# Pinning the splits of h between weight splits in the down projection, and spreading the turning of x2 over three steps

## The chip, the cores and the metric

The kernel runs on one core of a Trainium2 chip. The metric is the time of one execution in microseconds (us) of device time. Before the change it is 2275.61 us, the median of three runs (2274.94 to 2275.78). One further execution was taken with the hardware profiler; its trace is what the numbers of this document come from, unless a run is named.

## The reference, cut to what matters

One decoder layer on 512 tokens of width 2048: a mixing layer, cross attention to 256 memory tokens, and a SwiGLU feed-forward layer of width 5632. The change touches only the end of the last one:

```python
hf = rms_norm(x, g_ffn)
gg, uu = jnp.split(hf @ w_gu, 2, axis=-1)
return x + (jax.nn.silu(gg) * uu) @ w_down
```

Below, h is `silu(gg) * uu`, and x2 is the `x` that is added at the end.

## The kernel before, in words

**Products in three parts.** A matrix is split into a high part in fp32r and a low part, the rest (`split`, L159: ScalarE casts to the high part, VectorE subtracts it to get the low part). A product is then three matmuls: high by high, high by low, low by high (`mm3`). Each split of a 128x1024 tile costs one ScalarE and one VectorE instruction.

**The down projection.** It is computed with seven block products (a Strassen scheme on a 2 by 2 block matrix) in four steps, `STEPS = ((6,), (0, 3), (4, 5), (1, 2))`. Step 0 has one product, the others two each. A step runs over `NK = 22` values of `kp`; for each kp and each product it does four block pairs of three matmuls, so 12 matmuls per kp in step 0 and 24 in steps 1 to 3. The two first and the two last kp of a step are done together, block by block.

**Weights.** `load_w(step, kp)` issues the loads of a kp's weights on SyncE into one of three `raw` buffers and splits them into five `qh` (high) and four `ql` (low) buffers. In step 0 one call serves kp and kp + 1. It runs with priority `AHEAD = 150`: the planner that orders each engine's instructions ranks them as if they were written 150 instructions earlier. `done_split` holds the last weight split that was written.

**h.** The gate and up phases before leave h in DRAM, in `hd`, in 6 groups `GRP` of two 512-wide blocks (the last has one). A group serves four kp. `load_h(step, g)` has GpSimd load the group's combination for each product of the step into a `PB` buffer (there are 16), and `split_h(step, g)` splits it into two further PB buffers. If `SPLIT_AT` has an entry for the pair, the split isn't written with the load but later, in `late_splits`, right behind `load_w` of the step and kp of the entry; it must then be issued behind the last weight split written (`tc.issue_after`, an order on one engine without a wait). The last block of h is turned by `turn` in step 0, at kp 2 and 4 (VectorE transposes and sums, 32 small GpSimd writes to `hd`), and group 5 is loaded at kp 5.

Nothing but that lower limit and the priorities says where a late split of h goes in the engine's queue. An engine takes its instructions in the queue's order.

**x2.** The x that is added at the end lies in DRAM with features across partitions and has to be turned. It is done in 16 pieces: `load_piece` (SyncE load of 256 KB, which waits for the last weight split), `turn_piece` (a VectorE transpose behind the last weight split, then four GpSimd writes to `x2n`). `TURN_AT` lists the places; pieces are loaded two places ahead. `add_rows` adds rows of x2n into four 128x512 result tiles by GpSimd DMAs, at the places in `ROWS_AT`: columns 1024 to 2047 first, then the others.

Of the kernel before, what the change touches and what calls it, by code (L numbers as in the profile page):

```python
# [28 lines left out]
NK = NF // 2  # L29
# [31 lines left out]
def hybrid_block(ctx: ExitStack, tc: tile.TileContext, x_t, mem_t, sv, cmat, umask, w_a, w_r67, w_v, w_vg, w_v3,  # L61
# [26 lines left out]
    def bank(tag):  # L88
        return psp.tile([128, 512], F32, name=tag, tag=tag, bufs={"mm": 3, "s": 2, "t": 2, "o": 1}[tag])
# [66 lines left out]
    def split(hi, lo, src, gain=None):  # L156

        if gain is None:
            return S.copy(hi, src), V.tensor_sub(lo, src, hi)  # L159
        return (S.activation(hi, src, AF.Copy, scale=gain),  # L160
                V.scalar_tensor_tensor(lo, src, gain, hi, op0=OP.mult, op1=OP.subtract))
# [510 lines left out]
    done = set()  # L672
# [201 lines left out]
    w = Weights(w_r67, 4096)  # L874
# [205 lines left out]
    w = Weights(w_cq[1], 2048)  # L1080
# [7 lines left out]
    def sb1(tag, dt=F32):  # L1088
        return pool1.tile([128, COLS2.get(tag, 512)], dt, name=tag, tag=tag, bufs=BUFS2[tag])
# [7 lines left out]
    def split_cols(raw, a, n):  # L1097
        hi, lo = sb1("qh", F32R), sb1("ql", F32R)
        done_split[0] = split(hi[:, :n], lo[:, :n], raw[:, a:a + n])
        return hi, lo  # L1100
# [91 lines left out]
    def sb2(tag, dt=F32):  # L1192
        return pool2.tile([128, COLS2.get(tag, 512)], dt, name=tag, tag=tag, bufs=BUFS2[tag])
# [125 lines left out]
    def weights_a(kp):  # L1319
        p = kp + LAG  # L1320
        with tc.high_priority(offset=60):
            if p >= KP:
                if p not in both_raw:
                    both_raw[p] = raw = sb1("raw")
                    for i in range(2):
                        if kp + i < KP:
                            nc.sync.dma_start(raw[:, 1024 * i:1024 * i + 512], w_gu[0, kp + i, :, 1536:2048])
                            nc.sync.dma_start(raw[:, 1024 * i + 512:1024 * i + 1024], w_gu[0, kp + i, :, 0:512])
                            both_raw[p + i] = raw
                a = split_cols(both_raw[p], 1024 * ((p - KP) % 2), 1024)  # L1330
            else:
                a = split_cols(both_raw[p], 1024, 1024)
        return part(a, 0, 512), part(a, 512, 512)
# [61 lines left out]
    GRP = [range(g, min(g + 2, NB)) for g in range(0, NB, 2)]  # L1395
# [41 lines left out]
    for p in range(KP):  # L1437
        if 1 <= p < KP - 1:
            ws.append(co_weights(p + 1))
        if p >= LAG:  # L1440
            w = weights_a(p - LAG)
# [31 lines left out]
    quad = [(i, j) for i in range(2) for j in range(2)]  # L1473
    groups, dw = {}, {}

    SPLIT_AT = {(1, 3): (1, 6), (0, 2): (0, 4), (0, 3): (0, 6), (0, 4): (0, 10), (0, 5): (0, 18)}
    for s in (1, 2, 3):
        SPLIT_AT[s, 4], SPLIT_AT[s, 5] = (s, 10), (s, 14)
        if s > 1:
            SPLIT_AT[s, 0], SPLIT_AT[s, 1], SPLIT_AT[s, 2], SPLIT_AT[s, 3] = (s - 1, 18), (s, 2), (s, 4), (s, 6)  # L1480
    h_raw, h_split = {}, {}

    def split_h(step, g):
        n = 512 * len(GRP[g])
        for a in STEPS[step]:
            hi, lo = h_split.pop((a, g), None) or (sb2("PB", F32R), sb2("PB", F32R))
            split(hi[:, :n], lo[:, :n], h_raw.pop((a, g))[:, :n])
            groups[a, g] = hi, lo

    def load_h(step, g):  # L1490
        n = 512 * len(GRP[g])
        for a in STEPS[step]:
            raw = h_raw[a, g] = sb2("PB")
            r = 128 * SLOT[a] - 128
            G.dma_start(raw[:, :n], hd[g][r:r + 128])
            if step == 0:
                h_split[a, g] = sb2("PB", F32R), sb2("PB", F32R)
        if (step, g) not in SPLIT_AT:
            split_h(step, g)
# [81 lines left out]
    def late_splits(step, kp):  # L1581
        for (s, g), at in SPLIT_AT.items():
            if at == (step, kp):
                with tc.issue_after(done_split[0][0].ins), tc.issue_after(done_split[0][1].ins):
                    split_h(s, g)

    def load_w(step, kp):

        with tc.high_priority(offset=AHEAD):
            raw = sb1("raw")  # L1590
            x, y = raw[:, :1024], raw[:, 1024:]
            if step == 0:
                nc.sync.dma_start(x, w_down[3, kp])
                nc.sync.dma_start(y, w_down[3, kp + 1])
            elif step == 1:
                nc.sync.dma_start(x, w_down[0, kp])
                nc.sync.dma_start(y, tw.get((1, kp), w_down[1, kp]))
            elif step == 2:
                nc.sync.dma_start(raw, td[kp])
                x, y = y, x  # L1600
            else:
                nc.sync.dma_start(x, w_down[2, kp])
                nc.sync.dma_start(y, tw.get((3, kp), td[kp][:, 1024:]))
            w = [split_cols(raw, 0, 1024)]
            if step % 2 and (step, kp) not in tw:
                V.tensor_add(y, x, y)
            w.append(split_cols(raw, 1024, 1024))
            if step == 2:
                w.reverse()
            if step == 0:  # L1610
                dw[0, kp], dw[0, kp + 1] = w[:1], w[1:]
            else:
                dw[step, kp] = w
# [11 lines left out]
    x2n = dram.tile([T, D], F32, name="x2n", tag="x2n", bufs=1)  # L1625
    pieces = {}
    ORDER = [*range(8, KT), *range(8)]
    TURN_AT = [(step, kp) for step in (1, 2) for kp in range(2, 18, 2)]
    ROWS_AT = {(2, 3): ((0, 1), (1, 1)), (3, 3): ((0, 0), (1, 0))}

    def load_piece(p):
        if p < KT:
# [38 lines left out]
    def gather_all(*steps):  # L1671
        for s in steps:
            for x in range(4):
                gather(*s[:4], x, *s[4:])
# [6 lines left out]
    for step, plan in enumerate(STEPS):  # L1681
        rs_ = range(len(plan))
        if step == 0:
            banks[0] = banks[1]
        elif step == 1:
            banks = [[bank(t) for t in SETS[r]] for r in rs_]
        elif step == 2:
            banks[1] = [bank(t) for t in SETS[1]]
        else:
            banks = [[bank(t) for t in SETS[r]] for r in rs_]  # L1690
        at = 3 if step else 7
        for kp in range(NK):
            if step or kp % 2 == 0:
                load_w(step, kp)
                late_splits(step, kp)

            if kp in (1, NK - 1):
                for r in rs_ if kp == 1 or step == 2 else reversed(rs_):
                    for x in range(4):
                        for k in (kp - 1, kp):  # L1700
                            down_product(step, r, k, (x,))
                        if step == 3 and kp == NK - 1:
                            gather(ADD, *((0, 0), (1, 0))[r], banks[r], x, True, (r, x) == (0, 3))
            elif 1 < kp < NK - 2:
                for r in rs_:
                    down_product(step, r, kp, range(4))
            if step == 0 and kp in (2, 4):
                for go in turn(hs, NB - 1, kp // 2 - 1):
                    go()
            if step == 0 and kp == 5:  # L1710
                load_h(0, len(GRP) - 1)
            if (step, kp) in TURN_AT:
                p = TURN_AT.index((step, kp))
                for ahead in (0, 1, 2) if p == 0 else (2,):
                    load_piece(p + ahead)
                turn_piece(p)
            for which in ROWS_AT.get((step, kp), ()):
                add_rows(*which)
            if step < 3 and kp % 4 == 3 and kp >= at:
                load_h(step + 1, (kp - at) // 4)  # L1720
        if step == 0:
            load_h(1, len(GRP) - 2)
        if step < 3:
            load_h(step + 1, len(GRP) - 1)
        with tc.high_priority(offset=EVICT):
            if step == 0:
                for x in range(4):
                    S.copy(res[0, 1][x], banks[0][x])
            elif step == 1:
                for x in range(4):  # L1730
                    S.copy(res[1, 1][x], banks[1][x])
                gather_all((ADD, 0, 1, banks[1]))
                for x in range(4):
                    S.copy(res[0, 0][x], banks[0][x])
            elif step == 2:
                u = [sb2("C") for x in range(4)]
                for x in range(4):
                    S.copy(u[x], banks[0][x])
                gather_all((SUB, 0, 1, u))
                for x in range(4):  # L1740
                    ADD(u[x], u[x], banks[1][x])
        if step == 2:
            for x in range(4):
                store(x, 0, 1)
            gather_all((SUB, 1, 1, u, True))
            res[1, 0] = u
# [120 lines left out]
```

## Time and profile before

| | |
|---|---|
| median of three runs | 2275.61 us |
| profiled execution | 2274.64 us |
| its span in the trace | 2272.8 us |
| mean granted TensorE clock | 0.999 |
| TensorE's share of the chain that ended last | 94% |

The span runs from the program's first to its last instruction; the execution's time is 1.84 us longer. PE is TensorE, DVE VectorE, ACT ScalarE, POOL GpSimd, SP SyncE. A row of a timeline gives the start in us from the span's start, the duration, the engine, the line, what is written from what (a tile's name; PB<-PB is a split of h, qh<-raw and ql<-raw,qh are the two halves of a weight split, PB<-h is a load of h), how many instructions the row holds, and in brackets how long the engine was idle before and what ended that. A row of the waits gives us in total, how often, and the longest. PEclk is the granted share of TensorE's clock. The end of a matmul is modelled: one takes 0.39 us by its row and the next starts 0.23 us after it.

### The profile page before, as it was taken

To read this page: it belongs to the slowest core of one execution; us is meant where nothing else is said; L and a number is where in the kernel's file an instruction comes from. 1 tells how busy PE (TensorE), PEld (TensorE's weight loads), DVE (VectorE), ACT (ScalarE), POOL (GpSimd) and SP (SyncE) were. 2 spreads that over 40 slices of the span, in tenths; PEclk is the share of its full clock that TensorE was granted. 3 is DMA by queue.
4 is the path that set the end of the run, shared out by engine and by line. 5 is a ranking of instruction groups with operands and counts; after the bars stand their busy time and mean duration, and the time that the engine had idled before them with its cause. 6 is when DMAs were issued, how large, how long until landed. Compare 5 with 4: busy or idle time off the path is not lost.

```text
span 2272.8 us, 29839 instructions
## 1 busy us (share of the span) xinstructions
PE 2255.0 (99%) x10533; PEld 1869.5 (82%) x10533; DVE 1687.9 (74%) x2643; ACT 1157.5 (51%) x1759; POOL 441.8 (19%) x672
## 2 busy tenths in 40 slices
PE   9999999999999999999999999999999999999999
PEld 8988888888888888787888888888888877878887
DVE  6478865677785446698889888988898876776685
ACT  6334545566674336575555445544544545454452
POOL 0012100021110000110123323332333162223200
PEclk9999999999999999999999999999999999999999
DMA  6577656466645344595576657656765588899864
GB/s 199 137 190 183 168 158 175 126 169 176 153 165 187 131 138 137 195 247 177 170 208 199 177 178 207 199 172 180 209 195 173 174 286 297 294 290 318 285 220 148
DMA packets 136822, 442.60 MB, mean 195 GB/s; under 512 B 20160, under 2 KB 21184, under 8 KB 133728
## 3 DMA queue, kind: packets, MB, share of 16 engines
q1 hardware_dynamic: 82480, 306.83, 40.2%
q0 software_dynamic: 49440, 125.35, 22.7%
q10 hardware_dynamic: 4752, 8.52, 1.0%
q8 instruction: 82, 1.34, 0.2%
q14 instruction: 68, 0.56, 0.1%
HBM read 395.01 MB, written 98.30 MB: 217 GB/s over the span
## 4 chain that ended last, share of the span: by engine, by line
PE 94%; DMA 3%; DVE 2%; issue 1%; ACT 1%; POOL 0%; SPq 0%; DVEq 0%; ACTq 0%; POOLq 0%
PE mm L99 51%; PE t L99 17%; PE s L99 14%; PE o L99 10%; PE t L817 1%; DMA w<-w_c 1%; DMA PB<-h 1%; DMA h<-T 0%; DVE ql L159 0%; DMA w<-w_vsw 0%; DVE wl L159 0%; POOL h L1428 0%; ACT wh L159 0%; ACT qh L159 0%; DMA w<-w_a 0%
## 5 line engine op out<-in xcount | busy, mean ns | idle before, releaser
L159 ACT CAST qh<-raw 128x1024 fp32r<-128x1024 f32 (+1 forms) x526 | 510.9, 980 | 518.0 <-PE mm L99 130.8
L159 DVE TENSOR_TENSOR ql<-raw,qh 128x1024 fp32r<-128x1024 f32 (+1 forms) x526 | 589.3, 1129 | 129.5 <-PE mm L99 53.6
L99 PE MATMUL mm<-X,wh 128*128 128x512 f32 x1600 | 504.2, 395 | 0.0
L99 PEld LDWEIGHTS mm<-X,wh 128*128 128x128 f32 x1600 | 294.0, 188 | 56.3 <-issue 0.8
L99 PE MATMUL t<-qh,PB 128*128 128x512 f32 x968 | 333.3, 389 | 0.0
L99 PE MATMUL mm<-X,wl 128*128 128x512 f32 x800 | 313.6, 392 | 0.1
L99 PE MATMUL mm<-qh,PB 128*128 128x512 f32 x868 | 310.6, 391 | 1.7 <-ACT qh L159 0.9
L159 DVE TENSOR_TENSOR wl<-w,wh 128x1024 fp32r<-128x1024 f32 (+2 forms) x150 | 179.7, 1200 | 152.3 <-ACT wh L159 150.5
L159 ACT CAST wh<-w 128x1024 fp32r<-128x1024 f32 (+2 forms) x150 | 154.2, 1029 | 237.9 <-PE mm L99 174.8
L1428 POOL DMA_DIRECT2D h<-T x352 | 224.2, 702 | 218.8 <-DVE T L1408 175.4
L99 PE MATMUL s<-qh,PB 128*128 128x512 f32 x672 | 233.0, 392 | 7.0 <-ACT PB L159 4.2
L99 PE MATMUL mm<-qh,PA 128*128 128x512 f32 x640 | 219.9, 389 | 0.0
L99 PEld LDWEIGHTS t<-qh,PB 128*128 128x128 f32 x968 | 181.7, 188 | 37.9 <-ACT qh L159 0.2
L99 PEld LDWEIGHTS mm<-qh,PB 128*128 128x128 f32 x868 | 163.3, 188 | 37.2 <-ACT qh L159 2.3
L99 PE MATMUL t<-ql,PB 128*128 128x512 f32 x484 | 188.3, 389 | 0.0
L99 PE MATMUL o<-qh,PB 128*128 128x512 f32 x484 | 187.4, 389 | 0.0
L99 PEld LDWEIGHTS mm<-X,wl 128*128 128x128 f32 x800 | 150.2, 188 | 32.6 <-DVE wl L159 1.4
L99 PE MATMUL mm<-ql,PB 128*128 128x512 f32 x434 | 169.5, 391 | 0.1
L99 PEld LDWEIGHTS s<-qh,PB 128*128 128x128 f32 x672 | 126.1, 188 | 35.8 <-ACT PB L159 5.2
L99 PEld LDWEIGHTS mm<-qh,PA 128*128 128x128 f32 x640 | 120.2, 188 | 25.0
L99 PE MATMUL s<-ql,PB 128*128 128x512 f32 x336 | 131.2, 391 | 1.6 <-DVE ql L159 1.6
L99 PE MATMUL mm<-ql,PA 128*128 128x512 f32 x320 | 124.5, 389 | 0.0
(502 smaller groups left out, 3546.7 us busy)
## 6 DMA issues: line engine op xcount, KB each, us to landing
raw<-w_gu SPq DMA_DIRECT2D x88, 768.0 KB, 4.8
raw<-w_gu SPq DMA_DIRECT2D x88, 512.0 KB, 3.7
raw<-w_down SPq DMA_DIRECT2D x84, 512.0 KB, 5.3
td<-w_down POOLq DMA_DIRECT2D x66, 512.0 KB, 6.2
w<-w_a SPq DMA_DIRECT2D x60, 512.0 KB, 4.4
raw<-td SPq DMA_DIRECT2D x22, 1024.0 KB, 6.3
PB<-h POOLq DMA_DIRECT2D x35, 512.0 KB, 6.3
w<-w_out SPq DMA_DIRECT2D x32, 512.0 KB, 3.6
```

The lines of the kernel that those rows point to most:

```text
L99: last_mm[0] = PE.matmul(*args, **kw)
L159: return S.copy(hi, src), V.tensor_sub(lo, src, hi)
L817: PE.transpose(tp[:, 128 * (i - j):128 * (i - j) + 128], ps_[b][:, POFF[i] + 128 * j:POFF[i] + 128 * j + 128], ident)
L1428: queues[i].dma_start(rows[:, :, c:c + 32], src[32 * q:32 * q + 32, :, i])
```

## The change

1. `SPLIT_AT` places the splits of h for step 0: groups 2 to 5 now at kp 8, 12, 16 and 20, where they are first used (before: 4, 6, 10 and 18).
2. The weight split written next but one kp later (kp 10, 14, 18) must be issued behind that split of h, on ScalarE and on VectorE. Together with the existing `issue_after` this leaves the split of group 2 one place, between the weight splits of kp 9 and kp 10, and likewise for groups 3 and 4.
3. The loads of h for step 1 are written later in step 0: group 0 at kp 9 (before 7), group 1 at kp 17 (before 11), groups 2, 3 and 4 at the last kp (before 15, 19 and behind the loop).
4. The 16 pieces of x2 are turned at 5 places in step 1, 7 in step 2 and 4 in step 3 (before 8 and 8 in steps 1 and 2), and the rows are added at kp 12 of step 2 and kp 14 of step 3 (before kp 3 of each).

```diff
-    SPLIT_AT = {(1, 3): (1, 6), (0, 2): (0, 4), (0, 3): (0, 6), (0, 4): (0, 10), (0, 5): (0, 18)}
+    SPLIT_AT = {(1, 3): (1, 6), **{(0, g): (0, 4 * g) for g in range(2, len(GRP))}}
...
-    h_raw, h_split = {}, {}
+    h_raw, h_split, h_done = {}, {}, [None]
...
-            split(hi[:, :n], lo[:, :n], h_raw.pop((a, g))[:, :n])
+            done = split(hi[:, :n], lo[:, :n], h_raw.pop((a, g))[:, :n])
+            if step == 0:
+                h_done[0] = done
...
-            w = [split_cols(raw, 0, 1024)]
+            with ExitStack() as behind:
+                if step == 0 and (0, kp // 4) in SPLIT_AT and kp % 4 == 2:
+                    for i in h_done[0]:
+                        behind.enter_context(tc.issue_after(i.ins))
+                w = [split_cols(raw, 0, 1024)]
...
-    TURN_AT = [(step, kp) for step in (1, 2) for kp in range(2, 18, 2)]
-    ROWS_AT = {(2, 3): ((0, 1), (1, 1)), (3, 3): ((0, 0), (1, 0))}
+    TURN_AT = [(1, kp) for kp in range(4, 22, 4)] + [(2, kp) for kp in range(2, 21, 3)] + [
+        (3, kp) for kp in range(1, 11, 3)]
+    ROWS_AT = {(2, 12): ((0, 1), (1, 1)), (3, 14): ((0, 0), (1, 0))}
...
-        at = 3 if step else 7
...
-            if step < 3 and kp % 4 == 3 and kp >= at:
-                load_h(step + 1, (kp - at) // 4)
-        if step == 0:
-            load_h(1, len(GRP) - 2)
+            if step == 0:
+                for g in {9: (0,), 17: (1,), NK - 1: (2, 3, 4)}.get(kp, ()):
+                    load_h(1, g)
+            elif step < 3 and kp % 4 == 3:
+                load_h(step + 1, kp // 4)
```

## The prediction

> **What bounds the kernel now.** I read the page first, then busy time by stretches of the down projection, then TensorE's waits and its timeline, then the timelines of ScalarE, VectorE and GpSimd around each stall.
>
> ```profile
> span 2272.8 us, 29839 instructions
> PE 2255.0 (99%) x10533; PEld 1869.5 (82%) x10533; DVE 1687.9 (74%) x2643; ACT 1157.5 (51%) x1759; POOL 441.8 (19%) x672
> ```
> TensorE is the bound, so only its gaps can pay. The changed code runs from 1836.8 us on:
>
> ```profile
> core 0: us, PE busy (x) PEld busy (x) DVE busy (x) ACT busy (x) POOL busy (x), PEclk, DMA share, GB/s
> 1836.80:1858.50 21.70, 21.70 (x96) 17.67 (x95) 18.81 (x29) 10.14 (x11) 13.98 (x24) 1.00 1.02 364
> 1858.50:1874.50 16.00, 12.98 (x49) 10.05 (x48) 7.39 (x9) 5.16 (x5) 13.12 (x21) 0.89 0.74 199
> 1874.50:1888.60 14.10, 11.49 (x50) 9.09 (x50) 6.90 (x6) 7.08 (x8) 2.68 (x5) 1.00 0.77 283
> 1888.60:1906.30 17.70, 16.71 (x73) 13.22 (x72) 14.87 (x14) 11.59 (x13) 2.11 (x4) 1.00 0.79 292
> 1906.30:2026.00 119.70, 118.11 (x521) 97.47 (x521) 86.37 (x81) 56.20 (x60) 33.46 (x53) 1.00 0.85 292
> 2026.00:2146.00 120.00, 119.97 (x529) 98.68 (x528) 74.41 (x69) 60.08 (x62) 34.09 (x52) 1.00 0.90 298
> 2146.00:2260.00 114.00, 113.55 (x500) 93.32 (x499) 85.67 (x79) 51.18 (x51) 3.46 (x4) 1.00 0.60 205
> ```
> The first four rows are step 0; roughly, steps 1, 2 and 3 follow. TensorE idles 6.62 us in step 0 (3.02 + 2.61 + 0.99) and 1.59, 0.03 and 0.45 us in the others. The x2 part of the change lies in the stretches where little is lost. Here are the stalls of step 0:
>
> ```profile
> 1860.64 0.50 PE L99 MATMUL s<-qh,PB 128*128 128x512 f32 x1 [2.08 <-ACT PB L159]
> 1862.31 1.19 PE L99 MATMUL s<-qh,PB 128*128 128x512 f32 x2 [0.94 <-DVE PB L159]
> 1876.73 0.50 PE L99 MATMUL s<-qh,PB 128*128 128x512 f32 x1 [2.08 <-ACT PB L159]
> 1877.99 0.73 PE L99 MATMUL s<-qh,PB 128*128 128x512 f32 x2 [0.53 <-DVE PB L159]
> 1890.16 0.73 PE L99 MATMUL s<-qh,PB 128*128 128x512 f32 x2 [0.99 <-DVE PB L159]
> 1862.40:1865.80 3.40, 3.40 (x8) 2.72 (x9) 0.00 (x0) 0.00 (x0) 3.13 (x6) 0.50 0.95 313
> 1836.80 2.72 PE s L99 x12
> ```
> PB holds h. Twelve matmuls take 2.72 us undisturbed, so a pair of row blocks (kp k) would start at 1836.80 + 2.72k. I write w(k) for the split of its weights and h(s,g) for a group of h for step s; h(0,g) serves kp 4g to 4g+3. The stalls stand where h(0,2), h(0,3) and h(0,4) are first used. After the first, the granted clock is 0.50 for a stretch of 3.4 us.
>
> **Why h is late.** ScalarE's timeline, then one row of VectorE's, then GpSimd's:
>
> ```profile
> 1850.48 1.06 ACT L159 CAST qh<-raw 128x1024 fp32r<-128x1024 f32 x1 [1.71 <-DVE T L1418]
> 1853.15 1.06 ACT L159 CAST qh<-raw 128x1024 fp32r<-128x1024 f32 x1 [1.62 <-PE mm L99]
> 1858.59 1.04 ACT L159 CAST qh<-raw 128x1024 fp32r<-128x1024 f32 x1 [1.66 <-PE mm L99]
> 1859.54 1.04 ACT L159 CAST PB<-PB 128x1024 fp32r<-128x1024 f32 x1
> 1874.69 1.04 ACT L159 CAST qh<-raw 128x1024 fp32r<-128x1024 f32 x1 [1.66 <-PE mm L99]
> 1875.64 1.04 ACT L159 CAST PB<-PB 128x1024 fp32r<-128x1024 f32 x1
> 1882.90 1.05 ACT L159 CAST PB<-PB 128x1024 fp32r<-128x1024 f32 x1 [6.22 <-DMA PB<-h]
> 1883.86 1.05 ACT L159 CAST qh<-raw 128x1024 fp32r<-128x1024 f32 x1
> 1885.52 2.00 ACT L159 CAST PB<-PB 128x1024 fp32r<-128x1024 f32 x2 [0.61 <-DMA PB<-h]
> 1861.03 1.22 DVE L159 TENSOR_TENSOR PB<-PB 128x1024 fp32r<-128x1024 f32 x1
> 1842.81 1.11 POOL L1495 DMA_DIRECT2D PB<-h  x2
> 1847.65 0.53 POOL L1495 DMA_DIRECT2D PB<-h  x1 [3.73 <-PE mm L99]
> 1878.05 2.68 POOL L1495 DMA_DIRECT2D PB<-h  x5 [4.73 <-DMA h<-T]
> 1847.65 7.85 DMA PB<-h
> 1879.16 6.34 DMA PB<-h
> ```
> Five qh buffers let w(k) be cast only when kp k-5 is done. The cast at 1850.48 is therefore w(9) (kp 4 ends at 1850.40) and that at 1858.59 is w(12). h(0,2) stands behind w(12), at 1859.54, although it was issued at 1842.81 and, by the 7.85 us of h(0,4), had landed by about 1850.7. h(0,3) likewise stands behind w(16), at 1875.64. So the late thing is a place in ScalarE's queue, not a transfer. The third stall differs: h(0,4) is the second cast of the 1885.52 row, behind the two casts of h(1,0), of which the first held the queue 6.22 us for its transfer.
>
> **The sum, part by part.** The pins put h(0,2) between w(9) and w(10), h(0,3) between w(13) and w(14), h(0,4) between w(17) and w(18), on both engines. They add no instruction.
>
> Gain: idle time and the 3.4 us at half clock (worth 1.7 us) make 6.62 + 1.7 = 8.3 us. Restarts after a gap come on top, so I count matmuls: a matmul should take 2.72 / 12 = 0.2267 us, and one astride a seam between two windows is counted in both. The stretch of the first stall has 48 in 16.00 us, 16.00 - 10.88 = 5.1 us lost; the second 49 in 14.10, 14.10 - 11.11 = 3.0; the third 72 in 17.70, 17.70 - 16.32 = 1.4. Sum 9.5 us.
>
> Cover of the new places: w(9) ends at 1851.5 on ScalarE, h(0,2) follows for 1.04 us, before w(10) at 1853.15 is due, so that the added queueing costs w(10) nothing. VectorE subtracts w(9) when kp 5 is done (1853.1) and h(0,2) after it, 1.22 us each: done by 1855.6, needed at 1858.56, so 3.0 us to spare. The same sum holds for h(0,3) (needed at 1869.44), and for h(0,4), needed at 1880.32 and castable from about 1873.2, if h(1,0) is not ahead of it. w(10), w(14) and w(18) now wait behind h, and TensorE behind them; if a pinned h had not landed, each us of delay beyond 3.0 would cost a us. h(0,4) landed at 1855.50, long before.
>
> h(0,5), now behind w(21), is free when kp 17 is done, 1885.8, plus two subtractions: about 1888.2, against a need at 1891.20; its transfer, issued at 1878.05, by the 6.34 us of h(1,0)'s second one lands at 1884.4. Cover 3.0 us, cost 0.
>
> Moved loads: h(1,0) goes from kp 7 to kp 9. GpSimd issues it right behind h(0,5), which waits for block 10's writes to land (4.73 us), so its issue (second and third of the five at 1878.05) stays, and step 1 would begin at 1896.64, some 9 us after its two casts. h(1,1) is used 21.8 us into step 1 (four kp of 24 matmuls), h(1,2) and later 43 us and more: free. What is next late is h(1,0)'s first cast, landing at 1882.90, with w(18) or w(19) behind it: w(18) is due at 1885.76, and one cast and two subtractions end at 1882.90 + 1.05 + 2 x 1.22 = 1886.4, so 0.6 us lost; allowing as much again, I take 1.0.
>
> The x2 pieces:
>
> ```profile
> L1643 DVE STREAM_TRANSPOSE C<-C x16: 701/705/706, 1923.0 to 2111.3; 128x512 f32<-128x512 f32 x16
> L1647 POOL DMA_DIRECT2D x2n<-C x64: 649/649/710, 1924.0 to 2117.9; - x64
> L1652 POOL DMA_DIRECT2D C<-x2n x4: 849/1002/1382, 2147.7 to 2152.9; - x4
> DMA to landing us min/median/max: 4.6/9.3/17.7
> POOL x2n L1647 <- DVE C L1643: 106.3, 15, 15.4
> ```
> A piece is one SyncE load, a transpose of 0.705 us and four GpSimd writes of 0.649 us. GpSimd waits for each transpose, up to 15.4 us, with h's later loads behind; at 3 or 4 kp between pieces it can be 21.8 us, but a load written at kp 4g+3 is used at kp 4g of the next step, 19 kp (over 100 us) later. Four pieces enter step 3: 2.8 us of VectorE where it is busy 85.67 of 114 us, 10.4 us on an empty GpSimd. The load waits for the last weight split, and weight loads queue behind it on SyncE; three raw buffers cover that. The eight row additions of step 3 move to kp 14, about 2146 + 14 x 5.44 = 2222: eight issues of 1.0 us and 17.7 us to land give 2248, before kp 20 at 2254.8, where the last sums begin to need them. Step 2's additions, to kp 12, have 49 us. Cost 0, bounded by the one stall of step 1, 1.6 us, either way: it may go, as additions leave the start of step 2, or come again elsewhere.
>
> Sum: -9.5 + 1.0 + 0 = -8.5 us. The profiled execution took 2274.64 us (1.84 over its span), 0.97 under the median of 2275.61; from the median, 2267.1. Its own range, from -11.1 (no new delay, 1.6 us of step 1 too) to -5.5 (three us of cover lost), is 2264.5 to 2270.1. About 0.2%, 4.5 us, is what a measurement of this kernel can tell from no change.
>
> **The rivals.** *The stall moves to kp 16.* ScalarE keeps the order of the trace: h(1,0), w(17), h(1,0), h(0,4). For it: that order stands in the rows, h(1,0)'s load is still written ahead of h(0,4)'s split, and its transfer hangs on GpSimd, not on TensorE. Against: it arose while TensorE stood at h(0,3); without that stall w(17), h(0,4) and w(18) come free earlier, and the load is written two kp later. Then TensorE, free at 1880.32, waits for h(0,4) until the same 1887.5 and 1890.1 as now, gaining nothing, and a gap of 7 us would again bring 1.7 us of half clock in place of the old one, whose loss is absorbed: 0 to +1.7, so 2275.6 to 2277.3.
>
> [...]
>
> *The pins don't move the casts in time*: h(0,2)'s buffer is one that TensorE frees only when kp 7 ends. The row at 1859.54 shows no wait, but stands right behind one for TensorE, so this isn't excluded. No change, 2275.6.
>
> *Slower: both h(1,0) casts go ahead of w(14).* Deciding point: anything behind a cast that lands at 1885.50 (1879.16 + 6.34) and due before. w(14) would be cast at 1886.5 and subtracted by 1888.9, and kp 14, free at 1874.88, needs that for its second matmul: with half clock it starts in effect at 1888.9 - 0.2 + 1.7 = 1890.4. Now kp 16 starts in effect at 1890.16 - 0.45 = 1889.7 (the row is its third matmul), so kp 14 at 1889.7 - 1.4 - 5.44 = 1882.9. The third stall (1.4) would be gone: 7.5 - 1.4 = +6.1, so 2281.7. Against it: it needs the whole group to move up three weight splits.
>
> **How the numbers follow.** Forecast 0.60, stall moves to kp 16 0.22, pins idle 0.06, slower 0.12. Faster is the first, same the second and third, slower the last. The range 2264.5 to 2277.3 holds the first three, 0.88, less their tails.
>
> **What would show it.** Right: the first PB cast after 1850.48 follows w(9) directly and w(10) follows it; TensorE has no gap over 0.3 us between 1858 and 1880; the half clock stretch is gone; step 1's first matmuls come 8 to 9 us earlier. Wrong: a wait on PB near 1880 to 1890 with ScalarE waiting for PB<-h (the first rival), a wait of a PB cast for TensorE at 1858 (the second), or new idle time in steps 1 to 3 above 2 us.

## The result, and the profile after

The changed kernel is slower. Its median is 2288.22 us (2287.38 to 2291.08, five runs), against 2275.41 us (2274.94 to 2275.78, five runs) for the kernel before. The ratio is 1.0059, 95% interval 1.0044 to 1.0073. The forecast was 2267.1, and the range ended at 2277.3.

The profiled execution took 2288.06 us. Two lines of its page:

```profile
span 2286.3 us, 29838 instructions
PE 2255.3 (99%) x10533; PEld 1869.8 (82%) x10533; DVE 1686.7 (74%) x2643; ACT 1157.6 (51%) x1759; POOL 442.4 (19%) x672
```

TensorE's busy time and count are those of before (2255.0, 10533). The difference is idle time. Here are its waits from the start of the down projection to its end, first of the kernel before, then of the changed one (us in total, how often, the longest):

```profile
PE s L99 <- ACT PB L159: 4.2, 2, 2.1
PE s L99 <- DVE PB L159: 2.9, 4, 1.0
PE s L99 <- DVE ql L159: 1.6, 1, 1.6
```

```profile
PE s L99 <- ACT PB L159: 13.6, 1, 13.6
PE s L99 <- DVE PB L159: 3.7, 2, 2.3
PE mm L99 <- DVE ql L159: 1.7, 1, 1.7
```

Two waits for a cast of h have become one of 13.6 us, there is a new one for the low part of weights (`mm <- ql`), and the one of 1.6 us (`s <- ql`, between steps 1 and 2) is gone. Busy time by stretches shows where they lie; the down projection begins 3.33 us later than before, at 1840.13:

```profile
core 0: us, PE busy (x) PEld busy (x) DVE busy (x) ACT busy (x) POOL busy (x), PEclk, DMA share, GB/s
1840.13:1861.83 21.70, 21.70 (x97) 17.96 (x97) 21.28 (x34) 11.09 (x12) 13.93 (x24) 1.00 1.02 365
1861.83:1886.40 24.57, 10.95 (x50) 8.74 (x48) 4.58 (x4) 5.10 (x6) 15.17 (x25) 0.78 0.63 189
1886.40:1917.40 31.00, 29.64 (x120) 23.93 (x121) 21.44 (x20) 18.57 (x21) 2.12 (x4) 0.90 0.73 254
...
2157.00:2190.00 33.00, 29.01 (x127) 23.30 (x126) 23.23 (x24) 14.77 (x15) 8.73 (x12) 1.00 0.89 283
```

In the second row TensorE is busy 10.95 of 24.57 us; the last row, the first 33 us of step 3, has 4.0 us of idle time, where the kernel before had 0.45 us in the whole of step 3. ScalarE's timeline tells why step 0 stands still:

```profile
1853.81 1.06 ACT L159 CAST qh<-raw 128x1024 fp32r<-128x1024 f32 x1 [1.71 <-DVE T L1418]
1854.77 1.04 ACT L159 CAST PB<-PB 128x1024 fp32r<-128x1024 f32 x1
1856.49 1.06 ACT L159 CAST qh<-raw 128x1024 fp32r<-128x1024 f32 x1 [0.67 <-PE mm L99]
1859.21 1.06 ACT L159 CAST qh<-raw 128x1024 fp32r<-128x1024 f32 x1 [1.66 <-PE mm L99]
1861.93 1.06 ACT L159 CAST qh<-raw 128x1024 fp32r<-128x1024 f32 x1 [1.66 <-PE mm L99]
1882.13 1.04 ACT L159 CAST PB<-PB 128x1024 fp32r<-128x1024 f32 x1 [19.15 <-DMA PB<-h]
1883.09 1.04 ACT L159 CAST qh<-raw 128x1024 fp32r<-128x1024 f32 x1
1884.34 1.99 ACT L159 CAST PB<-PB 128x1024 fp32r<-128x1024 f32 x2 [0.22 <-DMA PB<-h]
```

The first row is w(9); h(0,2) follows it directly, then w(10), w(11) and w(12), as the pins say, and the first stall is gone. Behind w(12) stands h(1,0)'s first cast. It holds the queue for 19.15 us, until its data land. Only then come w(13), h(1,0)'s second cast and h(0,3), which kp 12 needs. GpSimd's timeline has the issue of that load, behind the writes of h's last block as before, and TensorE's timeline has the end of the wait:

```profile
1877.59 2.16 POOL L1497 DMA_DIRECT2D PB<-h  x4 [2.02 <-DMA h<-T]
```

```profile
1872.38 0.39 PE L99 MATMUL mm<-qh,PB 128*128 128x512 f32 x1
1886.39 0.79 PE L99 MATMUL s<-qh,PB 128*128 128x512 f32 x1 [13.62 <-ACT PB L159]
...
1888.97 1.22 PE L99 MATMUL s<-qh,PB 128*128 128x512 f32 x2 [1.36 <-DVE PB L159]
```

**A ledger of the down projection.** All these kernels execute the same 1848 matmuls of the down projection, in the same order but for 19 in the last two kp of step 0, so each matmul's start, counted from the first one of the down projection, can be compared with its start in the kernel before. The table gives that difference in us, for the changed kernel and all the experiments below, at six times of the kernel before: behind its three stalls (1874.0, 1888.6, 1906.3), at the end of step 1 and its stall (2026), before and behind the start of step 3 (2146, 2190), and at the end. "Starts" says how much later the down projection begins, where no edit here touches the code. Run 7 tells how far such numbers differ with no cause in the queues: up to 1.8 us.

| kernel | starts | 1874.0 | 1888.6 | 1906.3 | 2026 | 2146 | 2190 | end |
|---|---|---|---|---|---|---|---|---|
| the change | +3.33 | -5.21 | +9.24 | +7.76 | +6.20 | +6.19 | +10.10 | +10.09 |
| 1 without x2's part | +2.07 | -5.21 | +9.20 | +7.72 | +6.16 | +6.17 | +6.79 | +6.78 |
| 2 h(1,0) behind w(19) | +3.46 | -5.21 | -8.40 | -1.34 | -2.09 | -2.11 | -2.19 | -2.21 |
| 3 h(1,0) loaded early | +0.79 | -5.21 | -8.40 | -3.86 | -5.41 | -5.41 | -5.54 | -5.56 |
| 4 pins at the old places | +0.50 | -5.21 | -1.12 | +1.90 | +0.34 | +0.33 | +0.17 | +0.16 |
| 5 as 3, h(1,1) split later | +6.41 | -5.21 | -8.40 | -9.88 | -10.47 | -10.49 | -10.32 | -10.34 |
| 6 x2's part alone | +2.99 | +1.22 | +2.55 | +1.27 | -0.29 | -0.30 | +2.48 | +2.47 |
| 7 x2's additions alone (order as before) | +1.57 | +0.72 | +1.77 | +0.49 | -1.07 | -1.07 | -1.58 | -1.59 |
| 8 places without pins | +2.54 | -0.25 | +9.31 | +7.83 | +7.59 | +7.57 | +7.55 | +7.54 |
| 9 as 5, with x2's part | +2.54 | -5.21 | -8.40 | -9.88 | -9.75 | -9.77 | -6.14 | -6.16 |
| 10 as 3, h(1,1) loaded later | +1.18 | -5.21 | -8.40 | -9.88 | -11.42 | -11.43 | -10.82 | -10.83 |

For the changed kernel, 3.33 + 10.09 = 13.42 us is the whole difference of the two profiled executions (2288.06 - 2274.64). Step 0 gives 5.21 back, loses 14.45 (from -5.21 to +9.24) and ends at +7.76; step 3 loses 3.9 more.

### The profile page after: what moved, and what is told of

Its sections match the earlier page's. It is cut to its first block, busy times and chain, and to the rows that moved or that the text cites. A ratio compares the mean times of both kernels' runs of the same rounds, so it can differ in the third digit from the quotient of the medians.

```text
span 2286.3 us, 29838 instructions
## 1 busy us (share of the span) xinstructions
PE 2255.3 (99%) x10533; PEld 1869.8 (82%) x10533; DVE 1686.7 (74%) x2643; ACT 1157.6 (51%) x1759; POOL 442.4 (19%) x672
## 3 DMA queue, kind: packets, MB, share of 16 engines
q8 instruction: 82, 1.34, 0.2%
## 4 chain that ended last, share of the span: by engine, by line
PE 90%; DMA 3%; DVE 3%; issue 2%; ACT 1%; POOL 1%; SPq 0%; DVEq 0%; ACTq 0%; POOLq 0%
PE mm L99 50%; PE t L99 16%; PE s L99 13%; PE o L99 10%; DMA h<-T 1%; DMA PB<-h 1%; PE t L817 1%; POOL h L1428 1%; DVE wl L159 1%; DVE ql L159 1%; DMA raw<-w_down 0%; DMA w<-w_vsw 0%; ACT wh L159 0%; ACT qh L159 0%; DMA raw<-td 0%
## 5 line engine op out<-in xcount | busy, mean ns | idle before, releaser
L99 PE MATMUL s<-qh,PB 128*128 128x512 f32 x672 | 232.8, 391 | 17.3 <-ACT PB L159 13.6
```

The source lines that it names most:

```text
L99: last_mm[0] = PE.matmul(*args, **kw)
```

## The experiments

The theory after the result: what a split of h costs is set by what stands ahead of it on ScalarE, and h(1,0) came ahead of w(13) and h(0,3) because h(0,3)'s split is now written at kp 12, behind h(1,0)'s, which goes with its load at kp 9. (Before, it was written at kp 6, ahead of h(1,0) at kp 7, and stood ahead of it.) The rivals: the pins push weight splits back; the transfers are late in any order; the x2 part is what costs. Runs 1 to 4, 5 to 8, and 9 and 10 were each timed beside their own runs of the kernel before, whose medians were 2275.61, 2276.9 and 2275.06 us. Where the diff of a run doesn't say otherwise, it is against run 1.

**1. The change without x2's part.**

```diff
-    TURN_AT = [(1, kp) for kp in range(4, 22, 4)] + ...
-    ROWS_AT = {(2, 12): ((0, 1), (1, 1)), (3, 14): ((0, 0), (1, 0))}
+    TURN_AT = [(step, kp) for step in (1, 2) for kp in range(2, 18, 2)]
+    ROWS_AT = {(2, 3): ((0, 1), (1, 1)), (3, 3): ((0, 0), (1, 0))}
```

> The change without its x2 part: the pieces are turned and the rows added where they were before. Place theory (h(1,0)'s first cast stands on ScalarE behind w(12), ahead of w(13) and h(0,3), and holds them until its transfer lands near 1882 us): the 14 us gap at kp 12 and the half clock after it stay, ScalarE waits about 19 us for PB<-h; the time is the changed kernel's less what x2 costs there (about 2 us by the two traces: 3.9 lost in step 3, 1.9 gained between steps 1 and 2), so about 2286, 2283 to 2288. Rival (the x2 part with its transfers is what costs): near 2275 or below, and no such gap.

Measured: 2283.85 us, ratio 1.0033 (1.0022 to 1.0045). Step 0 is that of the changed kernel to 0.04 us. The loss at the start of step 3 shrinks from 3.9 us to 0.6. So the larger part of the loss is in step 0 and has nothing to do with x2.

**2. h(1,0) split at (0, 18).**

```diff
-    SPLIT_AT = {(1, 3): (1, 6), **{(0, g): (0, 4 * g) for g in range(2, len(GRP))}}
+    SPLIT_AT = {(1, 3): (1, 6), **{(0, g): (0, 4 * g) for g in range(2, len(GRP))}, (1, 0): (0, 18)}
```

> As e1, and one more entry places the split of h(1,0) behind w(19): only the place of two casts and two subtractions in their queues changes, no load moves. Place theory: no gap over 1.2 us in step 0, no half clock there; step 0 is 9.5 us shorter than before, at most 1 us given back where w(20) queues behind h(1,0): 2266 to 2268. Rival (the pins themselves hold the weight splits behind a late h): a gap of several us at kp 12 or 16 stays, 2280 or more.

Measured: 2273.96 us, ratio 0.9988 (0.9978 to 0.9997). The gap of 14 us is gone and so is the second stall (-8.40), with the pins in place: they aren't what costs. But the expected time is missed. ScalarE's timeline of this run:

```profile
1891.48 1.05 ACT L159 CAST PB<-PB 128x1024 fp32r<-128x1024 f32 x1 [9.33 <-DMA PB<-h]
1892.44 1.05 ACT L159 CAST qh<-raw 128x1024 fp32r<-128x1024 f32 x1
1893.94 2.00 ACT L159 CAST PB<-PB 128x1024 fp32r<-128x1024 f32 x2 [0.45 <-DMA PB<-h]
...
1898.69 0.61 ACT L159 CAST PB<-PB 128x512 fp32r<-128x512 f32 x1
```

The 128x512 cast is h(0,5), which kp 20 needs at about 1894.6; TensorE waits for it until 1899.35. Ahead of it stand h(1,0) and h(1,1), and the queue waited 9.33 us for the former to land. The same thing, one group further on.

**3. h(1,0) loaded at kp 1, split at (0, 10).** The load is now written ahead of the last block's writes to DRAM.

```diff
+    SPLIT_AT = {..., (1, 0): (0, 10)}
...
-                for g in {9: (0,), 17: (1,), NK - 1: (2, 3, 4)}.get(kp, ()):
+                for g in {1: (0,), 17: (1,), NK - 1: (2, 3, 4)}.get(kp, ()):
```

> As e1, but GpSimd loads h(1,0) at kp 1, ahead of the 32 writes of h's last block, and its split is placed behind w(11): its two casts keep a place ahead of w(13) and h(0,3) on ScalarE, yet their transfers land some 20 us earlier. Place theory (it is the wait for the transfer in that place that costs): the casts find their data, ScalarE waits for PB<-h under 2 us, no gap at kp 12; 2266 to 2270, with h(0,5) up to 2 us later. Rival (the place in itself, or the pins, cost whatever the transfer does): a gap of over 5 us stays, 2280 or more.

Measured: 2269.43 us, ratio 0.9969 (0.9955 to 0.9983). h(1,0) is still ahead, and costs nothing, because it has landed. What is left is a stall at kp 20; on ScalarE it is now h(1,1) that waits ahead of h(0,5), and 6.0 us are lost there, where the expectation allowed 2:

```profile
1889.42 1.05 ACT L159 CAST PB<-PB 128x1024 fp32r<-128x1024 f32 x1 [9.94 <-DMA PB<-h]
...
1893.21 0.61 ACT L159 CAST PB<-PB 128x512 fp32r<-128x512 f32 x1
```

**4. Pins with the splits at their old places** (4, 6, 10, 18); each group's pin is kept by its number.

```diff
-    SPLIT_AT = {(1, 3): (1, 6), **{(0, g): (0, 4 * g) for g in range(2, len(GRP))}}
+    SPLIT_AT = {(1, 3): (1, 6), (0, 2): (0, 4), (0, 3): (0, 6), (0, 4): (0, 10), (0, 5): (0, 18)}
...
-                h_done[0] = done
+                h_done[g] = done
...
-                    for i in h_done[0]:
+                    for i in h_done[kp // 4]:
```

> As e1, with the pins, but the splits of h for step 0 are written where they were before (kp 4, 6, 10, 18), so h(0,3) is written ahead of h(1,0). On ScalarE the first h(1,0) cast now stands behind w(16), the second behind w(17), then h(0,4). Place theory: the gaps at kp 8 and 12 go, and one at kp 16 takes their place (the first rival of the prediction): TensorE waits from 1880 until about 1887.5 and 1890, half clock again; 2275 to 2278. Rival (the pins cost in themselves): 2280 or more, gap at kp 12.

Measured: 2276.07 us, ratio 0.9999 (0.9991 to 1.0008). With h(0,3) written at kp 6 again, it stands ahead of h(1,0), and the second stall is gone too: TensorE has no gap at kp 12. (The table's -1.12 already holds most of the gap at kp 16, which begins at that very matmul; just before it the run stands at -8.40.) h(0,4), written at kp 10, is still behind h(1,0) at kp 9. ScalarE's timeline, h(1,0), w(17), then h(1,0) and h(0,4):

```profile
1883.38 1.04 ACT L159 CAST PB<-PB 128x1024 fp32r<-128x1024 f32 x1 [12.36 <-DMA PB<-h]
1884.33 1.04 ACT L159 CAST qh<-raw 128x1024 fp32r<-128x1024 f32 x1
1885.89 1.99 ACT L159 CAST PB<-PB 128x1024 fp32r<-128x1024 f32 x2 [0.52 <-DMA PB<-h]
```

This is the rival "the stall moves to kp 16" of the prediction, rows, place and price: nothing is gained.

**5. As run 3, with h(1,1) split at (1, 1)** and no longer at once with its load.

```diff
-    SPLIT_AT = {..., (1, 0): (0, 10)}
+    SPLIT_AT = {..., (1, 0): (0, 10), (1, 1): (1, 1)}
```

> This kernel is the change without its part on x2, with h(1,0) loaded at kp 1 and split at (0, 10) as in the run that loaded it early, and now also with h(1,1) split at (1, 1) and not at once. On ScalarE no cast of h(1,1) is then written ahead of the one of h(0,5). Theory (what counts is which cast of h stands ahead of which weight split): the gap at kp 20, which the early load left (2.2 us and 1.7 us of a half clock), goes as well, and all three stalls of step 0 are gone: 2275.6 - 9.5 = 2266.1, 2265 to 2268. Rival (the transfers of this stretch are the limit, so that whatever is split last is late in any order): a gap of 2 us or more stays at kp 16 or kp 20, and the time is that of the early load, 2269 to 2271.

Measured: 2269.21 us, ratio 0.9968 (0.9955 to 0.9981). The ledger has step 0 without any stall, 9.88 us shorter, and the down projection 10.34 us shorter; h(0,5) follows a weight split and waits for nothing:

```profile
1889.48 1.06 ACT L159 CAST qh<-raw 128x1024 fp32r<-128x1024 f32 x1 [1.66 <-PE mm L99]
1890.44 0.61 ACT L159 CAST PB<-PB 128x512 fp32r<-128x512 f32 x1
1892.20 1.06 ACT L159 CAST qh<-raw 128x1024 fp32r<-128x1024 f32 x1 [1.15 <-PE mm L99]
```

The theory holds for step 0. The time, 7.7 us under the median of before, is less than the down projection gained, no better than run 3's, and missed the expected 2265 to 2268. In the profiled execution the down projection began 6.41 us later, after a gap at 1571.00 to 1575.06 in which TensorE waited for weights of the gate and up phase. The changed kernel had such a gap at the same place (1571.53 to 1573.50), the kernel before and runs 1 to 4 had none.

**6. x2's part alone**, on the kernel before (the lines of run 1's diff, the other way round).

> The kernel before with only the change's part on x2: its pieces turned over steps 1 to 3, its additions at (2, 12) and (3, 14). The changed kernel stood 4.4 us above the change without this part (2288.2 and 2283.9). Theory (pieces and additions that meet the start of step 3 make the loads of weights land late there): the same cost shows alone, two gaps of 2 to 3 us at the start of step 3, some of it paid back by the gap between steps 1 and 2 that goes: 2277 to 2280. Rival (the cost arises only because step 0 ended later, with the writes of x2 then meeting other work): 2274.5 to 2276.5, no change.

Measured: 2277.96 us, ratio 1.0006 (0.9998 to 1.0015). The two gaps at the start of step 3 are there (+2.8 us from 2146 to 2190). The time is in the theory's range, but the interval goes from -0.5 to 3.4 us, so whether it costs time isn't settled by this run.

**7. x2's additions alone**, on the kernel before.

```diff
-    ROWS_AT = {(2, 3): ((0, 1), (1, 1)), (3, 3): ((0, 0), (1, 0))}
+    ROWS_AT = {(2, 12): ((0, 1), (1, 1)), (3, 14): ((0, 0), (1, 0))}
```

> The kernel before with only the places of x2's additions changed: (2, 12) and (3, 14) for (2, 3) and (3, 3); its pieces are turned where they were. If the additions are what delays the loads of weights at the start of step 3, this has the gaps of the whole x2 part there: 2277 to 2280. If the pieces that are turned and written in step 3 are what delays them, step 3 has no such gaps here, and the time is that of before or up to 2 us less (the 1.9 us gap between steps 1 and 2 may go with the additions): 2273.5 to 2276.

Measured: 2276.1 us, ratio 1.0001 (0.9991 to 1.001). No gap at the start of step 3 (-0.5 us). But the run doesn't test what it was meant to: the additions didn't move. TensorE, VectorE, GpSimd and SyncE execute the same instructions in the same order as in the kernel before, ScalarE too but for one swapped pair at 690 us; the additions stand here from 2020.9 to 2153.4 us, in the kernel before from 2020.4 to 2152.9. The entry in `ROWS_AT` alone doesn't decide their place. They do stand elsewhere in run 6, where the pieces are turned at other places. So it takes the pieces' new places, but whether by the pieces or by the additions that move with them, this run can't tell.

What it does show is how far two executions of the same order differ. The down projection begins 1.57 us later; step 0 has half clock for 10.24 us instead of 3.41 (up to +1.77 in the table); and the stall of 1.6 us between steps 1 and 2 isn't there (from +0.49 to -1.07). A single difference of that size in the table can't be put down to an edit.

**8. The places without the pins.**

```diff
-                if step == 0 and (0, kp // 4) in SPLIT_AT and kp % 4 == 2:
-                    for i in h_done[0]:
-                        behind.enter_context(tc.issue_after(i.ins))
+                pass
```

> The change without its part on x2 and without its pins: the splits are written at (0, 4g) and the loads of h(1,0) and h(1,1) at kp 9 and 17, but nothing ties them to weight splits. Theory (writing h(0,3)'s split at kp 12 puts it behind h(1,0)'s, which is written at kp 9, so that the new places bring h(1,0) forward): the gap before kp 13 is there without the pins too, and ends when the load of h(1,0) has landed, about where it ended with them, whether or not a gap at kp 8 comes first: 2282 to 2286. Rival (the pins push the weight splits behind h(1,0)): without them the stalls are those of the kernel before: 2274 to 2278.

Measured: 2284.3 us, ratio 1.0038 (1.0024 to 1.0052). ScalarE's timeline:

```profile
1861.14 1.04 ACT L159 CAST qh<-raw 128x1024 fp32r<-128x1024 f32 x1 [1.66 <-PE mm L99]
1862.09 1.04 ACT L159 CAST PB<-PB 128x1024 fp32r<-128x1024 f32 x1
1881.66 1.04 ACT L159 CAST PB<-PB 128x1024 fp32r<-128x1024 f32 x1 [18.54 <-DMA PB<-h]
```

Without the pins h(0,2) is behind w(12) again (-0.25: the first stall is back), and h(1,0) still comes next. The gap stands before kp 12 (the expectation puts it one kp late). The new places bring h(1,0) forward; the pins are what takes the first stall away.

**9. As run 5, with x2's part**, so the whole change with its two orders mended.

> The whole change, its part on x2 too, with h(1,0) loaded at kp 1 and split at (0, 10) and h(1,1) split at (1, 1). Step 0 without a stall, as in the run that has this without x2's part. Theory (x2's pieces that are written at the start of step 3 delay the weight loads there by 1.4 to 2 us twice, whatever step 0 does): two gaps at the start of step 3, 2.5 to 4 us more over the down projection than the kernel without x2's part, 2270 to 2274. Rival (the two gaps come only where step 0 ended late): no gaps in step 3, the time of the kernel without x2's part, 2267 to 2270.

Measured: 2268.33 us, ratio 0.9976 (0.9967 to 0.9985). The time is in the rival's range, below the theory's. The trace decides for the theory: the two gaps in step 3 are there once more (+3.6 us from 2146 to 2190, run 5: +0.2). They don't depend on how step 0 ends. What they cost in time stays open here too: run 5 has 0.9968, and the intervals overlap.

**10. As run 3, with h(1,1) loaded at kp 20** instead of 17, its split at once.

```diff
-                for g in {1: (0,), 17: (1,), NK - 1: (2, 3, 4)}.get(kp, ()):
+                for g in {1: (0,), 20: (1,), NK - 1: (2, 3, 4)}.get(kp, ()):
```

> The change without its part on x2, with h(1,0) loaded at kp 1 and split at (0, 10), and h(1,1) loaded at kp 20 and not at 17, its split following at once, behind the one of h(0,5). Theory (what counts is that no cast of h(1,1) stands ahead of h(0,5)'s): no stall in step 0 here either, as with h(1,1)'s split put off, 2266 to 2270. Rival (the later load of h(1,1) makes it late for kp 4 of step 1): a new gap of 1 to 3 us between 1900 and 1920, 2269 to 2273.

Measured: 2264.95 us (2263.36 to 2266.19), ratio 0.9955 (0.9943 to 0.9968): 1 us below the expected range, and the lowest median of all, 10.1 us under the kernel before and, by the two ratios, 1.0% under the changed one. Its interval overlaps with those of runs 3, 5 and 9. Its page, and all the waits of TensorE from the start of the down projection to 2260:

```profile
span 2263.2 us, 29840 instructions
PE 2251.9 (100%) x10533; PEld 1869.3 (83%) x10533; DVE 1688.0 (75%) x2643; ACT 1157.0 (51%) x1759; POOL 441.9 (20%) x672
```

```profile
PE s L99 <- DVE PB L159: 1.0, 1, 1.0
```

**What delays step 3.** Of the changed kernel: the row of the transfers for the weight load issued at 2160.76, the GpSimd issues beside it, and VectorE's wait. The columns of the first are size and us from issue to landing.

```profile
raw<-td SPq DMA_DIRECT2D x1, 512.0 KB, 11.7
```

```profile
2157.01 1.78 POOL L1659 DMA_DIRECT2D PA<-x2n  x2 [3.47 <-issue]
2158.13 1.53 POOL L1659 DMA_DIRECT2D C<-x2n  x1
2161.84 0.83 POOL L1659 DMA_DIRECT2D C<-x2n  x1 [2.18 <-DVE PA L1674]
2163.07 0.71 POOL L1654 DMA_DIRECT2D x2n<-C  x1 [0.39 <-DVE C L1650]
2164.03 1.97 POOL L1654 DMA_DIRECT2D x2n<-C  x3 [0.26 <-issue]
```

```profile
2172.53 1.23 DVE L1612 TENSOR_TENSOR raw<-raw 128x1024 f32<-128x1024 f32 x1 [7.52 <-DMA raw<-td]
```

The weight load takes 11.7 us. The same load in the kernel before, issued at 2151.24 and like this one 3.1 us behind the first matmul of step 3, takes 7.6:

```profile
raw<-td SPq DMA_DIRECT2D x1, 512.0 KB, 7.6
```

VectorE waited 3.52 us for it there. The next such load takes 11.5 us against 9.8. (Run 1 has 8.4 and 10.2.) So these weight loads aren't issued late; they take longer. The second gap in step 3, a wait for a subtraction of h, is 1.8 to 2.3 us in the three kernels with x2's part, and at most 1.0 us in the others.

Four of the eight additions written for kp 14 are issued at the start of step 3, as they are in run 1, where they are written for kp 3; counted from the first matmul of step 3, two of them come 3.7 us earlier than in run 1. New are a piece's four writes beside them. Runs 6 and 9 show that x2's part brings the gaps whatever step 0 does. Whether it is the piece's writes, its load, its 0.7 us on VectorE or the earlier additions was not tried apart.

## Why the prediction was wrong, point by point

**The sizes of the three stalls were right.** 5.1, 3.0 and 1.4 us were counted out of the matmuls; the ledger of runs 5 and 10 has 5.21, 3.19 and 1.48, together 9.88 for 9.5. The pins do what the prediction says, and the cover of w(9) to w(10) held: no weight split is late at kp 8 to 11.

**The step that failed** is "What is next late is h(1,0)'s first cast, landing at 1882.90, with w(18) or w(19) behind it", priced at 1.0 us. The landing was right (1882.13), and so was "its issue ... stays". What stands behind the cast was wrong: h(0,3), due at 1872.8, and w(13), due at 1875.5, and not w(18). That cost 14.45 us by the ledger, or 17.6 against runs 2 and 3, which pass the same place at -8.40. The prediction read the order of ScalarE's queue out of the trace of before and asked only how TensorE's earlier progress would shift it. But that order is in the program, and the change rewrites it: h(0,3)'s split moves from kp 6 to kp 12, past h(1,0)'s, which moves from kp 7 to kp 9. Runs 2 and 4 turn this order each in another way, and the gap moves with it, to kp 20 and kp 16. Run 8 keeps the order without the pins, and the gap stays at kp 12; run 3 keeps it with the data there in time, and the gap is gone. The trace of before had a hint: there h(0,4), written at kp 10, stood behind h(1,0), written at kp 7, and h(0,3), written at kp 6, ahead of it.

**The first rival** ("the stall moves to kp 16") was given 0.22. It describes run 4, the pins without the new places, to the row.

**The slower rival** had the right mechanism, a cast that waits for its load ahead of things due earlier, and 0.12. It put the cast ahead of w(14) and came to +6.1; it was ahead of w(13) and h(0,3), and step 0 ended 7.76 us late. What was held against it, "it needs the whole group to move up three weight splits", took the move for something that the timing would have to bring about; the edit of `SPLIT_AT` and of the loads' places does it by itself. In the traces ScalarE took its casts in the queue's order: at a cast of h without its data it stood idle for 19.15 us in the changed kernel and for 18.54, 12.36, 9.94 and 9.33 us in runs 8, 4, 3 and 2, and the weight split behind that cast then followed without a wait of its own.

**h(0,5)'s cover of 3.0 us** was worked out with nothing but weight splits ahead of it. In runs 2 and 3 h(1,0) and h(1,1) stood there; run 3 lost 6.0 us at kp 20 (from -8.40 to -3.86 by the ledger, and the third stall's 1.48, which went). With the order mended (runs 5 and 10) the cover is there.

**The x2 part was priced at nothing**, within 1.6 us either way. In the traces it costs 3.9, 2.8 and 3.6 us at the start of step 3 (the change, runs 6 and 9; all others lie between -0.5 and +0.6 there). The step that failed here is "weight loads queue behind it on SyncE; three raw buffers cover that". It asks when the loads can be issued; the late one was issued at its old place and took 11.7 us in place of 7.6. The eight additions of step 3 didn't all move to kp 14 either: four stayed at its start. The 1.6 us between steps 1 and 2 do go, but also without x2's part (runs 1, 3, 4 and 10) and in run 7, whose order is that of the kernel before, so they are no gain of it. In time the part costs less clearly: 1.0006 alone, 0.9976 against 0.9968 with the order mended, 4.4 us by the medians of the change and run 1.

**The half clock.** The prediction's rows show two gaps at the first stall, 2.08 and 0.94 us, with matmuls between them, and the half clock right after them. What the traces show of the half clock is in the last section; the size of the stall, 5.1 us, holds all the same.

**What stays open** is 2.7 us of the difference of 12.8: the down projection grew by 10.1. The rest arises before it, where the code is the same, above all in the gap at 1571. That gap is in the profiled executions of the change and of runs 5 and 8 and in none of the other nine. Whether these kernels bring it about, or whether it comes and goes between executions, the runs don't tell. A later start as such needs no cause in the kernel: run 7 has 1.57 us of it.

## What to carry to other kernels

When an edit moves instructions that share an in-order queue, write out the queue's new order from the places in the code before pricing anything, with the time at which each entry's data land; the order in the old trace holds only for the old places. An instruction that waits for a transfer belongs behind everything that is due before the transfer lands, or its load belongs early enough that it doesn't wait: each alone took the 14 us away here, and only both together took all the stalls. Price moved transfers by what they delay as well as by when they are done. And before reading an experiment, read in its trace whether the edit moved what it was meant to move.

## What the runs showed of the hardware

In the kernel before, the half clock after the first stall lasted 3.41 us. In the changed kernel TensorE stops at 1872.8, and the records have the lower clock from 1875.3 to 1892.4, 17.06 us or five times 3.41, 6 us past the restart; runs 2, 3 and 4 have 6.83, 3.41 and 10.24 us, two, one and three times that. In the view by stretches of the changed kernel:

```profile
1872.77:1875.34 2.57, 0.00 (x0) 0.00 (x0) 0.00 (x0) 0.00 (x0) 2.57 (x5) 1.00 0.47 102
1875.35:1892.41 17.06, 4.66 (x10) 3.26 (x11) 6.99 (x6) 6.82 (x7) 2.91 (x6) 0.50 0.63 211
1892.42:1900.00 7.58, 7.58 (x35) 6.23 (x35) 4.81 (x4) 4.44 (x5) 0.00 (x0) 1.00 0.64 205
```

Since 11 of its 17 us lie under the gap, it adds little: the 10 matmuls of the second row take 4.66 us in place of 2.27 (at 0.2267 us each), so about 2.4 us beside a gap of 14.

TensorE didn't stand still all the time ahead of the half clock. In the 3.41 us just before it, it was busy 0.80 us in the kernel before and 0.84 in the changed one:

```profile
1858.96:1862.37 3.41, 0.80 (x3) 0.36 (x3) 3.26 (x6) 1.62 (x2) 2.66 (x5) 1.00 0.87 187
```

```profile
1871.93:1875.34 3.41, 0.84 (x4) 0.38 (x2) 0.00 (x0) 0.00 (x0) 3.41 (x6) 1.00 0.44 96
```

In the kernel before, 2.47 us between the starts of two matmuls, with 1.34 us between two others soon after, were followed by the half clock at the first stall; 2.47 and 0.92 us, at the second, weren't (1.00 in the prediction's row from 1874.50), nor were 2.47 us alone in run 9 (at 2167.58) or 2.70 us alone in the changed kernel (at 2184.38). The order of the instructions doesn't settle it: run 7 has that of the kernel before, with 10.24 us of half clock in step 0 for 3.41 there. What decides whether a gap brings the half clock wasn't shown.
